# Spreading a delta-rule head's log decays by broadcast transfers instead of TensorE products

## The chip, the cores and the metric

The kernel runs on one core of a Trainium2 chip. The metric is the device time of one execution in microseconds (us). The engines are named as in the profile: PE is TensorE, PEld its weight loads, DVE is VectorE, ACT is ScalarE, POOL is GpSimd and SP is SyncE, which here only issues transfers.

## The reference, cut to what matters

A trunk of two layers on x of 512 tokens by 1024 channels: layer 0 mixes tokens with a bidirectional gated delta rule (GDN), layer 1 with gated linear attention (GLA), and each is followed by an MLP; all of it in float32. The change is in the GDN layer. Per head (8 heads, keys and values of 128) and per direction, in chunks of the sequence:

```python
gc = jnp.cumsum(g.reshape(bn, h, n, CHUNK), axis=-1)          # log decays, summed in the chunk
causal = jnp.tril(jnp.ones((CHUNK, CHUNK), bool))
decay_mat = jnp.exp(jnp.where(causal, gc[..., :, None] - gc[..., None, :], -jnp.inf))
a_mat = jnp.where(strict, jnp.einsum('bhncd,bhnsd->bhncs', kb, k) * decay_mat, 0.0)
lhs = a_mat + jnp.eye(CHUNK, dtype=F32)
sol = lax.linalg.triangular_solve(lhs, rhs, left_side=True, lower=True, unit_diagonal=True)
...
qk = jnp.einsum('bhncd,bhnsd->bhncs', q, k) * decay_mat
q_dec = q * jnp.exp(gc)[..., None]
```

What the change concerns is `decay_mat` and `exp(gc)`: for both, the 512 summed log decays of a direction, which lie one to a token, must be had along the free axis on all 128 partitions, that is spread.

## The kernel before, in words

The tokens are treated as 4 blocks of 128 (NT = 4), both directions side by side, so that one head has U = 8 blocks of 128x128. Projections keep float32 accuracy by three products on TensorE: weights and x are split in a high part (`wh`, `xth`, written by ACT) and a low part (`wl`, `xtl`, by DVE).

`gdn` (L1337) walks the heads in a software pipeline. In iteration i it traces `recur` of head i-2, `solve` of head i-1, `project` of head i and `finish` of head i-2. A scheduler then orders the instructions of every engine's queue from the traced program by what each needs and by priority; an engine's queue is executed strictly in that order. `issue_after` puts an instruction behind another one in this order.

`project` (L1423) makes the four projections of a head (k, q, v, z) and their short convolutions (`conv`, ACT and DVE); after k and q comes `rows` (L1463). There PE transposes k and q blocks (`ktp`), ACT takes sums of squares (`junk`) and the logarithm `lnr`, and DVE makes `rw`, the log decay row of each token and direction (L1488). DVE splits `rw` into three bf16 parts (`rsp`, L1490 to L1496), PE transposes these in four blocks (`rtp`, L1499), and ACT copies the result to `rt`, 6 partitions by 512 (L1501).

`solve` (L1519) begins with the k by k products (`kk`) and, per direction, a product of a constant selector `sel` with `rt` (`ep`, L1534), which spreads the row over 128 partitions in PSUM. ACT takes its exponential as `qd` (L1536) and DVE multiplies it by q. A second product per direction (L1549) adds to the same `ep` the constant triangle `mi` of zeros and very negative numbers; ACT takes `E`, the decay matrix, as eight exponentials from it (L1553), each with a bias per token (`cj`). DVE multiplies E by `kk` (`at`, L1555), ACT rounds it to fp16 (`ath`, L1557).

Then the inverse: 4x4 blocks by three small rounds (`hp`, L1569, with `dc`), their transposes (`xp`, L1585; `Xd`, L1587), and five levels of doubling, 4 to 64. At each level PE makes three sets of eight products `lv` (L1614): one set from `ath` and `Dd`, which ACT or DVE copies to `pz` (L1628 up to 32, L1644 at 64), and two with `pz`, from which `Dd` and `Xd` are updated; at the last level by two ACT copies into `Dd` (L1649) and two of DVE into `Xd` (L1651). Each set waits for the one before. Then comes a correction step (`nw`, L1660 and L1661), the q by k products, and `qke`, E times these.

`recur` (L1687) runs the chunk recurrence with `m` products (L1708), on ACT `vd` (L1723), `vn` (L1726) and `sn` (L1734), and ends with the output products `op`, which use `qke` and `qd`. `finish` (L1749) normalises them (`fo`, L1762) and transposes (`otp`).

SP's queue carries the weights, 512 KB a transfer. In this stage POOL works only at the start, on constant masks (L1170).

Of the kernel before, what the change touches and what calls it, by code (L numbers as in the profile page):

```python
# [17 lines left out]
P = 128  # L18
S = 512
D = 1024  # L20
KT = D // P
NT = S // P
# [1096 lines left out]
NEG = -1e30  # L1119


class GdnConst:


    def __init__(self, c, pool, w_in, w_g, a_log, dt_bias, conv_w, norm_g, x):
        self.c, self.pool = c, pool
# [43 lines left out]
    def masks(self):  # L1170
        c, pool = self.c, self.pool
        G = c.nc.gpsimd
        self.idb = pool.tile([P, P], BF16, name="idb", bufs=1)
        G.tensor_copy(self.idb, c.ident)
        self.idh = pool.tile([P, P], F16, name="idh", bufs=1)
        G.tensor_copy(self.idh, c.ident)

        sf = pool.tile([6, 2, P], F32, name="self", tag="E", bufs=2)
        G.memset(sf, 0.0)
        for s in range(3):  # L1180
            G.affine_select(out=sf, in_=sf, compare_op=ALU.not_equal, fill=1.0, base=-2 * s,
                            pattern=[[-1, 2], [0, P]], channel_multiplier=1)
        self.sel = pool.tile([6, 2, P], BF16, name="sel", bufs=1)
        G.tensor_copy(self.sel, sf)
        self.mi = [pool.tile([P, P], BF16, name=f"mi{d}", bufs=1) for d in range(2)]
        for d in range(2):
            t = pool.tile([P, P], F32, name="tri", tag="cf", bufs=2)
            self.tri(t, d, False, 0.0, NEG)
            G.tensor_copy(self.mi[d], t)

        self.nd = pool.tile([P, P], F32, name="nd", bufs=1)
        G.tensor_scalar(self.nd, c.ident, -1.0, 1.0, ALU.mult, ALU.add)
# [144 lines left out]
def gdn(c, w_in, conv_w, a_log, dt_bias, norm_g, w_out, ln_g, ln_b, x, xt, w_next):  # L1337
    tc, nc = c.tc, c.nc
    w_in, w_g = w_in
    with c.banks(ch=2, pj=3, tp=1, ac=2), tc.tile_pool(name="gdn", bufs=1) as pool:  # L1340
        g = GdnConst(c, pool, w_in, w_g, a_log, dt_bias, conv_w, norm_g, xt)
# [9 lines left out]
        def load_z(hf):  # L1351
            if hf:
                tl = pool.tile([P, NT, S], F32, name="z", tag="sil", bufs=3)
            else:
                tl = heads[-1].next.kq
                more = [heads[-1].t2(tag, n).rearrange("p n i -> p (n i)") for tag, n in (("kt", 3), ("qd", 4))]
# [30 lines left out]
class GdnHead:  # L1387
# [30 lines left out]
    def new_tile(self):  # L1418
        self.sil = self.pool.tile([P, 4, S], F32, name="sil", tag="sil", bufs=3)
        self.kq = self.sil[:, 2:4, :]  # L1420
        return self.sil[:, 0:2, :]

    def project(self, done):  # L1423

        c, pool, g, h = self.c, self.pool, self.g, self.h
# [4 lines left out]
        for i, ci in enumerate((A_H + h, h, 2 * A_H + h, 3 * A_H + h)):  # L1430
            if h == 0 and i == 0:
                ps = g.k0
            else:
                with g.then() if h == 0 else contextlib.nullcontext():
                    wh, wl = c.wcols(self.w_in, ci * P)
                ps = c.bank([P, S], F32, name="pj" + "kqvz"[i], tag="pj")
                for k in range(KT):
                    c.mm3(ps, wh[:, k, :], wl[:, k, :], c.xth[:, k, :], c.xtl[:, k, :], k == 0, k == KT - 1)
                    if h == 0 and (i, k) == (3, 6):
                        g.sums()  # L1440
                        yield from rows
# [12 lines left out]
            yield 0.69, 0.0  # L1454
            if i == 1:
                rows = self.rows(done)
                if h:
                    yield from rows
                else:
                    next(rows)  # L1460
                    next(rows)

    def rows(self, done):  # L1463
# [18 lines left out]

        rw = c.small.tile([P, NT, 2], F32, name="rw", tag="rw")
        self.cj = cj = c.small.tile([P, NT, 2], F32, name="cj", tag="cj")
        lnk = lnr[:, 0, :].unsqueeze(2).to_broadcast([P, NT, 2])
        V.scalar_tensor_tensor(rw, lnk, -0.5, g.gc[:, :, :, h], ALU.mult, ALU.add)  # L1488

        rs = c.small.tile([P, NT, 6], BF16, name="rsp", tag="rsp")  # L1490
        r1 = c.small.tile([P, NT, 2], F32, name="r1", tag="r1")
        V.tensor_copy(rs[:, :, 0:2], rw)
        V.tensor_tensor(r1, rw, rs[:, :, 0:2], ALU.subtract)
        V.tensor_copy(rs[:, :, 2:4], r1)
        V.tensor_tensor(r1, r1, rs[:, :, 2:4], ALU.subtract)
        V.tensor_copy(rs[:, :, 4:6], r1)  # L1496
        rtp = self.bank("rtp", BF16, tag="tp")
        for n in range(NT):
            T.transpose(rtp[:6, n, :], rs[:, n, :], g.idb)  # L1499
# [19 lines left out]
    def solve(self, done):  # L1519
# [8 lines left out]
            T.matmul(kk[:, n, :], self.kc(n), self.kc(n), start=True, stop=True)  # L1528
        yield 0.9, 0.3

        eps, self.qd = [], []
        for d in range(2):
            ps = self.bank("ep")
            T.matmul(ps, g.sel[:, d, :], self.rt, start=True, stop=True)  # L1534
            x = self.t2("qd", 4)
            A.activation(x, ps, AF.Exp)  # L1536
            V.tensor_tensor(x, self.kq[:, 1, :].rearrange("p (n i) -> p n i", n=NT), x, ALU.mult)
            self.qd.append(x)
            eps.append(ps)
        yield 0.63, 1.4  # L1540

        ath, atl = t8("ath", 1), t8("atl", 1)
        kks = self.t2("on", 2)
        V.tensor_tensor(kks, kk, g.nd.unsqueeze(1).to_broadcast([P, NT, P]), ALU.mult)
        a4 = t8("a4", 1)
        ex, ats = [], []
        with c.in_order(mybir.EngineType.PE):
            for d in (1, 0):
                T.matmul(eps[d], g.idb, g.mi[d].unsqueeze(1).to_broadcast([P, NT, P]), start=False, stop=True, skip_group_check=True)  # L1549
        for d, ps in enumerate(eps):  # L1550
            e = self.t2("E", 2)
            for n in range(NT):
                A.activation(e[:, n, :], ps[:, n, :], AF.Exp, bias=self.cj[:, n, d:d + 1])  # L1553
# [92 lines left out]
        ps = prod(xd, pd, 64, 0)  # L1646
        px = prod(pd, xd, 64, 1)
        for d in range(2):
            A.copy(dd[row(1 - d), dirs[d], row(d)], ps[row(1 - d), d, :, :])  # L1649
# [37 lines left out]
    def recur(self, done):  # L1687
# [51 lines left out]
        self.op = op = self.bank("op", tag="ch")  # L1739
        for n in (1, 2, 0, 3):  # L1740
            mm = [(self.qke[d][:, n, :], vns[d][n]) for d in range(2)]
            mm += [(self.qd[d][:, n, :], states[d][n]) for d in range(2) if states[d][n] is not None]
# [103 lines left out]
```

## Time and profile before

| | us |
|---|---|
| three runs | 1327.30, 1327.93, 1328.49 |
| median | 1327.93 |
| profiled execution, its own time | 1328.52 |
| its span in the profile | 1326.6 |
| delta-rule stage with its preparation, in the span | from the start to about 410 |

The trace is of one execution; the span runs from its first instruction to its last, and the 1.9 us between it and the execution's own time lie around it. "Busy" counts an engine's instructions, and PE's matmuls are pipelined, so that each is recorded longer than the step to the next one; a product's cost on PE is therefore read from start to start. In a group's row the numbers behind the bar are busy time, mean ns of one instruction, and idle time before with its releaser.

### The profile page before, as it was taken

The page shows a single profiled execution, that of the slowest core. Times are in us where ns is not written, and L with a number is a line of the kernel's source. Part 1 is how long each engine was busy: PE and PEld are TensorE (multiplying, and loading weights), DVE is VectorE, ACT ScalarE, POOL GpSimd, SP SyncE. Part 2 cuts the span into 40 slices and gives each one's busy share as a digit, 9 for nine tenths or more (in the row PEclk, how much of TensorE's full clock was granted, in tenths as well). Part 3 has the DMA queues.
Part 4 walks back from the last instruction along what each step waited for, and adds up shares of the span by engine and source line. Part 5 has one row for each costly group of instructions (what it writes and reads, how often), then busy time and mean ns, then how long its engine had stood idle before and what let it go on. Part 6 is the DMA issues. An engine that isn't in the chain of part 4 may idle for free.

```text
span 1326.6 us, 22309 instructions
## 1 busy us (share of the span) xinstructions
PE 1307.4 (99%) x8659; PEld 1113.2 (84%) x8659; DVE 1107.7 (83%) x1823; ACT 805.2 (61%) x1598; POOL 124.8 (9%) x177
## 2 busy tenths in 40 slices
PE   9999999999999999999999999999999999999996
PEld 7777877787777889999998888888889889999985
DVE  7787888888668988989988787967879789989887
ACT  4757666767643666566667754654456466666656
POOL 5000000000000910101102200000001001101021
PEclk9999999999999999999999999999999999999998
DMA  5210120211222585675648521111216465657465
GB/s 181 96 49 33 49 65 33 64 49 57 73 99 85 189 178 154 156 191 153 151 150 170 149 90 64 65 63 64 95 64 213 105 193 154 149 172 161 142 143 143
DMA packets 44045, 154.36 MB, mean 116 GB/s; under 512 B 5419, under 2 KB 5795, under 8 KB 43939
## 3 DMA queue, kind: packets, MB, share of 16 engines
q1 hardware_dynamic: 32163, 110.85, 24.9%
q0 software_dynamic: 11776, 42.08, 16.1%
q8 instruction: 68, 1.11, 0.3%
q14 instruction: 38, 0.31, 0.1%
HBM read 113.99 MB, written 2.10 MB: 88 GB/s over the span
## 4 chain that ended last, share of the span: by engine, by line
PE 92%; ACT 3%; DVE 3%; issue 1%; DVEq 0%; POOL 0%; ACTq 0%; POOLq 0%
PE fx L128 3%; PE fx L130 3%; PE fx L129 3%; PE pX L130 3%; PE pX L129 3%; PE pX L128 3%; PE pjv L128 3%; PE pjv L129 3%; PE pjv L130 3%; PE m L1708 3%; PE fyz L128 3%; PE fyz L129 3%; PE fyz L130 3%; PE pY L129 2%; PE pY L128 2%; PE pY L130 2%
## 5 line engine op out<-in xcount | busy, mean ns | idle before, releaser
L102 ACT CAST wh<-wst 128x1024 fp32r<-128x1024 f32 x152 | 159.4, 1049 | 110.3 <-PE fyz L129 35.3
L107 DVE TENSOR_TENSOR wl<-wst,wh 128x1024 fp32r<-128x1024 f32 x150 | 184.3, 1229 | 42.2 <-ACT wh L102 41.9
L107 DVE TENSOR_TENSOR w2l<-w2r,w2h 128x1024 fp32r<-128x1024 f32 x92 | 112.3, 1221 | 24.0 <-ACT w2h L102 23.8
L102 ACT CAST w2h<-w2r 128x1024 fp32r<-128x1024 f32 x94 | 98.5, 1048 | 47.4 <-PE pX L130 16.2
L415 POOL DMA_DIRECT2D w2r<-w2r x56 | 48.5, 892 | 493.9 <-DVE w2l L107 247.3
L102 ACT CAST ah<-h 128x1024 fp32r<-128x1024 f32 x56 | 58.9, 1052 | 40.8 <-PE pX L129 18.1
L464 DVE TENSOR_TENSOR wst<-wst 128x512 f32<-128x512 f32 x120 | 79.8, 685 | 0.4
L107 DVE TENSOR_TENSOR al<-h,ah 128x1024 fp32r<-128x1024 f32 x56 | 68.3, 1220 | 5.1 <-ACT ah L102 4.8
L130 PE MATMUL pX<-w2h,al 128*128 128x512 f32 x168 | 66.2, 394 | 0.0
L129 PE MATMUL pX<-w2l,ah 128*128 128x512 f32 x168 | 66.1, 393 | 0.0
L128 PE MATMUL pX<-w2h,ah 128*128 128x512 f32 x168 | 65.8, 392 | 0.0
L128 PE MATMUL pjv<-wh,xth 128*128 128x512 f32 x128 | 54.7, 427 | 0.0
L128 PE MATMUL fx<-xth,wh 128*128 128x256 f32 x192 | 53.6, 279 | 0.0
L130 PE MATMUL fx<-xh,wl 128*128 128x256 f32 x192 | 53.6, 279 | 0.0
L130 PE MATMUL fyz<-xh,wl 128*128 128x256 f32 x192 | 53.6, 279 | 0.0
L128 PE MATMUL fyz<-xh,wh 128*128 128x256 f32 x192 | 53.6, 279 | 0.0
L128 PE MATMUL fx<-xh,wh 128*128 128x256 f32 x192 | 53.5, 278 | 0.0
L129 PE MATMUL fx<-xl,wh 128*128 128x256 f32 x192 | 53.5, 278 | 0.0
L130 PE MATMUL fx<-xth,wl 128*128 128x256 f32 x192 | 53.4, 278 | 0.0
L129 PE MATMUL fx<-xtl,wh 128*128 128x256 f32 x192 | 53.4, 278 | 0.0
L129 PE MATMUL fyz<-xl,wh 128*128 128x256 f32 x192 | 53.4, 278 | 0.0
L129 PE MATMUL pj<-xtl,wh 128*128 128x256 f32 (+1 forms) x160 | 52.0, 326 | 0.2 <-DVE xtl L194 0.2
(538 smaller groups left out, 4320.7 us busy)
## 6 DMA issues: line engine op xcount, KB each, us to landing
wst<-in_w SPq DMA_DIRECT2D x68, 512.0 KB, 4.3
w2r<-in_w SPq DMA_DIRECT2D x60, 512.0 KB, 4.0
w2r<-w2r POOLq DMA_DIRECT2D x56, 512.0 KB, 5.3
wst<-in_a_in SPq DMA_DIRECT2D x32, 512.0 KB, 3.3
wst<-in_b_vr SPq DMA_DIRECT2D x16, 512.0 KB, 3.3
wst<-in_a_out SPq DMA_DIRECT2D x8, 512.0 KB, 3.3
wst<-in_b_in SPq DMA_DIRECT2D x8, 512.0 KB, 3.3
wst<-in_b_out SPq DMA_DIRECT2D x8, 512.0 KB, 3.3
```

The source lines that it names most:

```text
L102: h = nc.scalar.copy(hi, src)
L107: self.halves = h, nc.vector.tensor_tensor(lo, src, hi.bitcast(F32), ALU.subtract)
L128: mm(ps, ah, bh, start=start, stop=False, **kw)
L129: mm(ps, ah, bl, start=False, stop=False, **kw)
L130: self.last_mm = mm(ps, al, bh, start=False, stop=stop, **kw)
L415: nc.gpsimd.dma_start(blocks[a + (q,)], blocks[b + (q,)], accum_op=ALU.add)
L464: plus = lambda a, b: V.tensor_tensor(a, a, b, ALU.add)
L1708: T.matmul(ps[:, d, :], *ops(d), start=True, stop=True)
```

## The change

The bf16 split, the selector products and the mask products go, with their constants (`idb`, `sel`, `mi`). The two triangles of 0 and very negative numbers are made once in float32 (`later`) and written four times side by side to DRAM (`laterd`) by POOL's queue at the start. Per head:

- SP's queue loads `E` (two directions by 512 per partition, float32) from `laterd`, after the q projection.
- PE makes one float32 transpose of `rw` (`rtp`, 8 partitions by 128), ACT copies it to `rt`, and ACT's queue writes `rt` to DRAM (`row`, 4 KB).
- POOL's queue adds `row`, broadcast to all 128 partitions, to `E` (an accumulating transfer), and then writes the same broadcast into `qd`.
- The eight exponentials of `E` work in place in SBUF. For all heads but the first they are put behind `solved`, the last `Dd` copy of the previous head.
- The exponentials of `qd` and the multiplication by q are traced later, behind the copy of `Xd`.
- The convolutions of k and q, the Silu, and `rows` get a higher priority in the scheduler (`soon`) for all heads but the first.

Buffers: `E` keeps two slots for two heads (both directions in one tile), `qd` likewise; before, `E` had two slots of one direction.

```diff
@@ masks
-        self.idb = pool.tile([P, P], BF16, name="idb", bufs=1)
-        G.tensor_copy(self.idb, c.ident)
...
-        self.mi = [pool.tile([P, P], BF16, name=f"mi{d}", bufs=1) for d in range(2)]
+        later = pool.tile([P, 2, P], F32, name="later", bufs=1)
         for d in range(2):
-            t = pool.tile([P, P], F32, name="tri", tag="cf", bufs=2)
-            self.tri(t, d, False, 0.0, NEG)
-            G.tensor_copy(self.mi[d], t)
+            self.tri(later[:, d, :], d, False, 0.0, NEG)
+        self.later = self.dram.tile([P, 2, NT, P], F32, name="laterd", bufs=1)
+        for n in range(NT):
+            G.dma_start(self.later[:, :, n, :], later)
@@ GdnHead
+    def soon(self, n=350):
+        return self.c.tc.high_priority(offset=n) if self.h else contextlib.nullcontext()
@@ project
             if i < 3:
-                self.conv(kq[:, i, :] if i < 2 else self.v, ps, ci)
+                with self.soon(250) if i < 2 else contextlib.nullcontext():
+                    self.conv(kq[:, i, :] if i < 2 else self.v, ps, ci)
...
-                c.exp_ln_after(A.activation(t, t, AF.Silu))
+                with self.soon():
+                    c.exp_ln_after(A.activation(t, t, AF.Silu))
             yield 0.69, 0.0
             if i == 1:
+                self.e = pool.tile([P, 2, NT, P], F32, name="E", tag="E", bufs=2)
+                c.nc.sync.dma_start(self.e, g.later)
                 rows = self.rows(done)
                 if h:
-                    yield from rows
+                    with self.soon():
+                        yield from rows
@@ rows
-        V.tensor_copy(rs[:, :, 0:2], rw)
-        V.tensor_tensor(r1, rw, rs[:, :, 0:2], ALU.subtract)
-        V.tensor_copy(rs[:, :, 2:4], r1)
-        V.tensor_tensor(r1, r1, rs[:, :, 2:4], ALU.subtract)
-        V.tensor_copy(rs[:, :, 4:6], r1)
-        rtp = self.bank("rtp", BF16, tag="tp")
-        for n in range(NT):
-            T.transpose(rtp[:6, n, :], rs[:, n, :], g.idb)
-        self.rt = pool.tile([6, S], BF16, name="rt", tag="rt", bufs=2)
-        A.copy(self.rt, rtp[:6, :, :].rearrange("p n i -> p (n i)"))
+        rtp = self.bank("rtp", shape=(2 * NT, P), tag="tp")
+        T.transpose(rtp, rdn.rearrange("p d n -> p (d n)"), c.ident)
+        rt = pool.tile([2 * NT, P], F32, name="rt", tag="rt", bufs=2)
+        A.copy(rt, rtp)
+        row = g.dram.tile([2 * NT, P], F32, name="row", tag="row", bufs=3)
+        self.qd = pool.tile([P, 2, NT, P], F32, name="qd", tag="qd", bufs=2)
+        c.nc.scalar.dma_start(row, rt)
+        every = row.rearrange("u p -> (u p)").partition_broadcast(P)
+        c.nc.gpsimd.dma_start(self.e.rearrange("p d n i -> p (d n i)"), every, accum_op=ALU.add)
+        c.nc.gpsimd.dma_start(self.qd.rearrange("p d n i -> p (d n i)"), every)
@@ solve
-        for d in range(2):
-            ps = self.bank("ep")
-            T.matmul(ps, g.sel[:, d, :], self.rt, start=True, stop=True)
-            x = self.t2("qd", 4)
-            A.activation(x, ps, AF.Exp)
-            V.tensor_tensor(x, self.kq[:, 1, :].rearrange("p (n i) -> p n i", n=NT), x, ALU.mult)
...
-        with c.in_order(mybir.EngineType.PE):
-            for d in (1, 0):
-                T.matmul(eps[d], g.idb, g.mi[d].unsqueeze(1).to_broadcast([P, NT, P]), start=False, stop=True, skip_group_check=True)
-        for d, ps in enumerate(eps):
-            e = self.t2("E", 2)
-            for n in range(NT):
-                A.activation(e[:, n, :], ps[:, n, :], AF.Exp, bias=self.cj[:, n, d:d + 1])
+        for d in range(2):
+            e = self.e[:, d, :, :]
+            with c.tc.issue_after(self.solved.ins) if h else contextlib.nullcontext():
+                for n in range(NT):
+                    A.activation(e[:, n, :], e[:, n, :], AF.Exp, bias=self.cj[:, n, d:d + 1])
...
         A.copy(xd, xp)
+        for d in range(2):
+            x = self.qd[:, d, :, :]
+            A.activation(x, x, AF.Exp)
+            V.tensor_tensor(x, self.kq[:, 1, :].rearrange("p (n i) -> p n i", n=NT), x, ALU.mult)
...
-            A.copy(dd[row(1 - d), dirs[d], row(d)], ps[row(1 - d), d, :, :])
+            self.next.solved = A.copy(dd[row(1 - d), dirs[d], row(d)], ps[row(1 - d), d, :, :])
```

How the queues move is read from the order of each engine's instructions in the built program; line numbers behind the change are its own. The first place is PE's queue in one head of the pipeline before, at the products that spread and mask (`m_...` are the recurrence's, `pjq` the next head's q projection):

```order
L1534 MATMUL ep<-rt,sel 128x512
L128 MATMUL pjq<-xth,wh 128x512
L129 MATMUL pjq<-xtl,wh 128x512
...
L1534 MATMUL ep<-rt,sel 128x512
...
L1549 MATMUL ep<-mi_304,idb 128x512
L1708 MATMUL m_2275<-vd,kt 128x128
...
L1549 MATMUL ep<-mi_303,idb 128x512
```

With the change none of these four stands in PE's queue. In their place is one transpose per head, which stands among the levels of the previous head. From it to that head's first `nw` PE has, in head 3, 23 projection products of 512 columns, 9 products of 128 columns and 64 level products; heads 4, 5 and 6 have the same numbers. In head 0 it has 48 projection products and 4 `kk` between the transpose and the first `hp`. The beginning and the end of head 3's piece:

```order
L130 MATMUL pjz<-xth,wl 128x512
L128 MATMUL pjz<-xth,wh 128x512
L1494 MATMUL rtp<-ident,rw 8x128
L129 MATMUL pjz<-xtl,wh 128x512
...
L1758 MATMUL otp<-ident,fo 128x128
L129 MATMUL pjk<-xtl,wh 128x512
L130 MATMUL pjk<-xth,wl 128x512
...
L1652 MATMUL nw<-Dd,ath 128x128
```

So the row is made before the previous head's inverse is finished, where before it was made at about that inverse's end. The third place is ACT's queue in a head of the middle. Before, from the last level of the head in `solve` on:

```order
L1644 ACTIVATE pz_141<-lv 64x4x64
L1649 CAST Dd<-lv 64x4x64 x2
L1501 COPY rt<-rtp 6x512
L1696 COPY vt<-ktp 128x512
L102 CAST wh<-wst 128x1024
L1762 ACTIVATE fo<-op,ors 128x128 x4
L1536 ACTIVATE qd<-ep 128x512 x2
L1723 ACTIVATE vd<-m_2264,kds 128x128
```

and with the change (`pz_143` is the last level's buffer, `pz_141` the one before it):

```order
L1496 COPY rt<-rtp 8x128
L1499 DMA row<-rt 8x128
L102 CAST wh<-wst 128x1024
L1620 CAST pz_141<-lv 32x4x32 x4
...
L1688 COPY vt<-ktp 128x512
...
L1636 ACTIVATE pz_143<-lv 64x4x64
L1578 ACTIVATE qd<-qd 128x512
L1754 ACTIVATE fo<-op,ors 128x128
L1641 CAST Dd<-lv 64x4x64 x2
L1754 ACTIVATE fo<-op,ors 128x128 x3
L1541 ACTIVATE E<-E,cj 128x128 x8
```

The copy of `rt` moves from behind the `Dd` copies to ahead of the last two levels; one exponential of `qd`, which needs POOL's second transfer of the new head, now stands ahead of the previous head's `Dd` copies, and the eight of `E` stand in one block behind them. Heads 3 to 6 have this order. In head 2 the first `qd` exponential stands ahead of `pz_141`; in head 1 both stand behind `E`; in head 7 the first stands ahead of `Dd` again, behind a Silu with its two table loads, and PE has 30 products of 512 columns between its transpose and `nw`. On POOL the two transfers of each head follow one another, with nothing between them.

More of the change, by code (lines that the diff above doesn't have):

```diff
@@ L1122, with __init__ @@
 class GdnConst:
-    def __init__(self, c, pool, w_in, w_g, a_log, dt_bias, conv_w, norm_g, x):
-        self.c, self.pool = c, pool
+    def __init__(self, c, pool, dram, w_in, w_g, a_log, dt_bias, conv_w, norm_g, x):
+        self.c, self.pool, self.dram = c, pool, dram
         nc = c.nc
@@ L1172, in masks @@
         G = c.nc.gpsimd
-        self.idb = pool.tile([P, P], BF16, name="idb", bufs=1)
-        G.tensor_copy(self.idb, c.ident)
         self.idh = pool.tile([P, P], F16, name="idh", bufs=1)
         G.tensor_copy(self.idh, c.ident)
[L1178 to L1184, printed above, removed]
-        self.mi = [pool.tile([P, P], BF16, name=f"mi{d}", bufs=1) for d in range(2)]
+        later = pool.tile([P, 2, P], F32, name="later", bufs=1)
         for d in range(2):
-            t = pool.tile([P, P], F32, name="tri", tag="cf", bufs=2)
-            self.tri(t, d, False, 0.0, NEG)
-            G.tensor_copy(self.mi[d], t)
+            self.tri(later[:, d, :], d, False, 0.0, NEG)
+        self.later = self.dram.tile([P, 2, NT, P], F32, name="laterd", bufs=1)
+        for n in range(NT):
+            G.dma_start(self.later[:, :, n, :], later)
         self.nd = pool.tile([P, P], F32, name="nd", bufs=1)
@@ L1339, in gdn @@
     w_in, w_g = w_in
-    with c.banks(ch=2, pj=3, tp=1, ac=2), tc.tile_pool(name="gdn", bufs=1) as pool:
-        g = GdnConst(c, pool, w_in, w_g, a_log, dt_bias, conv_w, norm_g, xt)
+    with c.banks(ch=2, pj=3, tp=1, ac=2), tc.tile_pool(name="gdn", bufs=1) as pool, \
+            tc.tile_pool(name="gdr", bufs=1, space=bass.MemoryType.DRAM) as dram:
+        g = GdnConst(c, pool, dram, w_in, w_g, a_log, dt_bias, conv_w, norm_g, xt)
         hi = [c.big.tile([P, 2, S], F32R, name=f"oh{t}", tag=f"xt{t}") for t in range(NT)]
@@ L1355, in load_z @@
                 tl = heads[-1].next.kq
-                more = [heads[-1].t2(tag, n).rearrange("p n i -> p (n i)") for tag, n in (("kt", 3), ("qd", 4))]
+                more = [heads[-1].t2("kt", 3).rearrange("p n i -> p (n i)"),
+                        pool.tile([P, 2, S], F32, name="qd", tag="qd", bufs=2)[:, 0, :]]
             for t in range(NT):
@@ L1481, in rows @@
         A.activation(lnr, ssp, AF.Ln, bias=c.bias[RMS_EPS])
-        rw = c.small.tile([P, NT, 2], F32, name="rw", tag="rw")
+        rdn = c.small.tile([P, 2, NT], F32, name="rw", tag="rw")
+        rw = rdn.rearrange("p d n -> p n d")
         self.cj = cj = c.small.tile([P, NT, 2], F32, name="cj", tag="cj")
@@ L1488, in rows @@
         V.scalar_tensor_tensor(rw, lnk, -0.5, g.gc[:, :, :, h], ALU.mult, ALU.add)
-        rs = c.small.tile([P, NT, 6], BF16, name="rsp", tag="rsp")
-        r1 = c.small.tile([P, NT, 2], F32, name="r1", tag="r1")
-        V.tensor_copy(rs[:, :, 0:2], rw)
-        V.tensor_tensor(r1, rw, rs[:, :, 0:2], ALU.subtract)
-        V.tensor_copy(rs[:, :, 2:4], r1)
-        V.tensor_tensor(r1, r1, rs[:, :, 2:4], ALU.subtract)
-        V.tensor_copy(rs[:, :, 4:6], r1)
-        rtp = self.bank("rtp", BF16, tag="tp")
-        for n in range(NT):
-            T.transpose(rtp[:6, n, :], rs[:, n, :], g.idb)
-        self.rt = pool.tile([6, S], BF16, name="rt", tag="rt", bufs=2)
-        A.copy(self.rt, rtp[:6, :, :].rearrange("p n i -> p (n i)"))
+        rtp = self.bank("rtp", shape=(2 * NT, P), tag="tp")
[8 more added lines that the diff above has]
+        c.nc.gpsimd.dma_start(self.qd.rearrange("p d n i -> p (d n i)"), every)
         V.scalar_tensor_tensor(cj, lnk, -0.5, g.lg[:, :, :, h], ALU.mult, ALU.add)
@@ L1741, in recur @@
             mm = [(self.qke[d][:, n, :], vns[d][n]) for d in range(2)]
-            mm += [(self.qd[d][:, n, :], states[d][n]) for d in range(2) if states[d][n] is not None]
+            mm += [(self.qd[:, d, n, :], states[d][n]) for d in range(2) if states[d][n] is not None]
             for i, (l, r) in enumerate(mm):
```

4 lines of the change are left out of this document (removed).

## The prediction

> **What bounds the kernel now.** I read the page's busy shares and chain first, to see which engine sets the end.
>
> ```profile
> span 1326.6 us, 22309 instructions
> PE 1307.4 (99%) x8659; PEld 1113.2 (84%) x8659; DVE 1107.7 (83%) x1823; ACT 805.2 (61%) x1598; POOL 124.8 (9%) x177
> PE 92%; ACT 3%; DVE 3%; issue 1%; DVEq 0%; POOL 0%; ACTq 0%; POOLq 0%
> ```
>
> PE is busy 99% of the span and is 92% of the chain that ended last. The change touches only the delta-rule stage, so its share is read from windows inside that stage (columns: time, then PE, weight load, DVE, ACT and POOL busy, granted clock, DMA share, GB/s) and from PE's waits over the whole of it, 18 to 420 us.
>
> ```profile
> 220.00:260.00 40.00, 39.66 (x367) 32.22 (x366) 32.97 (x74) 27.50 (x81) 0.00 (x0) 1.00 0.13 41
> 260.00:300.00 40.00, 39.86 (x360) 31.75 (x359) 33.25 (x73) 25.83 (x76) 0.00 (x0) 1.00 0.16 54
> ...
> PE lv L1614 <- ACT pz L1628: 1.7, 6, 0.4
> PE nw L1660 <- ACT Dd L1649: 0.8, 2, 0.6
> ```
>
> About one head passes per 40 us. PE lacks work for 0.1 to 0.3 us of it, at the full granted clock; the two largest of the named waits make 2.5 us in 400, both on ACT. POOL does nothing there and the transfer engines are at 0.13 to 0.16. So PE time that is taken away should come out of the end, and any wait put into ACT's queue ahead of a level of the inverse comes into it.
>
> **The products that go.** PE's timeline of one head (start, duration; I take start to start, since products overlap):
>
> ```profile
> 210.78 0.39 PE L129 MATMUL pjq<-xtl,wh 128*128 128x512 f32 x1
> 211.10 0.39 PE L1499 MATMUL rtp<-idb,rsp 128*6 128x128 bf16 x4
> 211.42 0.50 PE L130 MATMUL pjq<-xth,wl 128*128 128x512 f32 x1
> 211.76 0.39 PE L128 MATMUL pjq<-xth,wh 128*128 128x512 f32 x1
> 211.98 0.40 PE L129 MATMUL pjq<-xtl,wh 128*128 128x512 f32 x1
> ...
> 212.46 0.60 PE L1694 MATMUL ktp<-ident,sil 128*128 128x128 f32 x4
> 212.99 0.60 PE L1534 MATMUL ep<-rt,sel 6*128 6x512 bf16 x2
> 213.52 0.50 PE L128 MATMUL pjq<-xth,wh 128*128 128x512 f32 x1
> 213.85 0.40 PE L129 MATMUL pjq<-xtl,wh 128*128 128x512 f32 x1
> ...
> 214.98 0.59 PE L1549 MATMUL ep<-mi,idb 128*128 128x512 bf16 x2
> 215.22 0.58 PE L130 MATMUL pjq<-xth,wl 128*128 128x512 f32 x1
> 215.64 0.40 PE L128 MATMUL pjq<-xth,wh 128*128 128x512 f32 x1
> ```
>
> The four transposes hold 211.10 to 211.42, 0.32 us; the two spreading products 212.99 to 213.52, 0.53; the two mask products 214.98 to 215.22, 0.24. Together 1.09 us. A plain projection product takes 0.22 (211.76 to 211.98; elsewhere 0.23); beside the removed ones they take 0.32, 0.34, 0.33 and 0.42 (from 210.78, 211.42, 213.52 and 215.22), which is 0.53 more. If all of that goes too, it is 1.62. I take 1.4 a head, 11.2 us for eight. One new f32 transpose per head costs a quarter of the four at 212.46 (0.53 to the next start), 0.13, so 1.0 for eight. **The gain is 10.2 us, from 7.7 to 12.** The five small DVE instructions a head that go with the split are worth nothing by themselves: DVE has 7 us of 40 idle and PE, not DVE, is short; were that cover gone, five at about the 0.21 us of ACT's small `neg` below would be 1 us a head.
>
> **The transfers that come.** They replace something that took one PE product and no transfer, and the trace of before has none like them. Per head ACT's queue writes 4 KB to DRAM (`row`), then POOL issues an accumulating broadcast of 512 KB into E and one of 512 KB into qd. Nearest rows (issues in POOL's timeline, landings in the transfer view of 689 to 697 us, KB and us; then the page):
>
> ```profile
> 691.31 0.57 POOL L614 DMA_DIRECT2D ln<-in_ln_b  x1 [40.02 <-PE fyz L130]
> ...
> ln<-in_ln_b POOLq DMA_DIRECT2D x1, 512.0 KB, 4.2
> ln<-in_ln_g POOLq DMA_DIRECT2D x1, 512.0 KB, 5.0
> gst<-in_b_gates SPq DMA_DIRECT2D x1, 128.0 KB, 2.1
> ...
> w2r<-w2r POOLq DMA_DIRECT2D x2, 512.0 KB, 7.1
> ...
> L415 POOL DMA_DIRECT2D w2r<-w2r x56 | 48.5, 892 | 493.9 <-DVE w2l L107 247.3
> w2r<-w2r POOLq DMA_DIRECT2D x56, 512.0 KB, 5.3
> out<-xt SPq DMA_DIRECT2D x4, 256.0 KB, 3.5
> ```
>
> Call X the time from the issue of `row` to the landing of qd. The small transfer takes 2.1 (`gst`, a read) to 3.5 (`out`, a write of 64 times the bytes); I take 2.4, since 4 KB is nearer to the first. POOL's issue of the accumulating one takes 0.57 to 0.89; I take 0.9. The second of a pair from POOL landed after 5.0; 4.2 is the first, 5.3 the accumulating kind. So X is 2.4 + 0.9 + 5.0 = 8.3 us, at least 2.1 + 0.57 + 4.2 = 6.9, at most 3.5 + 0.9 + 5.3 = 9.7.
>
> The page "DMA: Bandwidth & Descriptors" of the Trainium skill, section "Anatomy of one DMA — SWDGE (gpsimd) path", fits a POOL transfer as about 2.0 us plus the bytes over 436 GB/s; that is an estimated 3.2 us for 512 KB, against 4.2 to 5.3 in the rows above, and by it X would be about 6.1 and everything hidden. The same section says that the receipt is slowest where the target is DRAM, which speaks against the trip of `row`; no run here shows such a small write yet.
>
> **What waits for them.** In ACT's new order for heads 3 to 6, `qd<-qd` and one `fo` stand ahead of the last level's two `Dd` copies, and PE's `nw` of the head before needs `Dd`. ACT's prices (us busy, mean ns) and PE's stretch there:
>
> ```profile
> L1762 ACT ACTIVATE fo<-op,ors 128x128 f32<-128x128 f32 x32 | 9.3, 372 | 2.9 <-DVE ors L211 2.8
> L1536 ACT ACTIVATE qd<-ep 128x512 f32<-128x512 f32 x16 | 9.3, 612 | 8.2 <-PE ep L1534 8.2
> L1553 ACT ACTIVATE E<-ep,cj 128x128 f32<-128x128 f32 x64 | 18.9, 404 | 3.8 <-PE ep L1549 3.8
> L1649 ACT CAST Dd<-lv 64x256 f16<-64x256 f32 x16 | 5.9, 367 | 2.7 <-PE lv L1614 2.3
> L1505 ACT ACTIVATE neg<-rw 128x8 f32<-128x8 f32 x8 | 1.7, 209 | 3.7 <-DVE rw L1488 3.6
> ...
> 197.51 0.39 PE L129 MATMUL pjz<-xtl,wh 128*128 128x512 f32 x1
> 198.20 0.39 PE L1614 MATMUL lv<-pz,Xd 128*128 128x64 f16 x8 [0.30 <-ACT pz L1628]
> 198.43 0.40 PE L1614 MATMUL lv<-Xd,pz 128*128 128x64 f16 x8
> ...
> 200.46 0.40 PE L130 MATMUL pjz<-xth,wl 128*128 128x512 f32 x1
> 201.23 0.66 PE L1473 MATMUL ktp<-ident,sil 128*128 128x128 f32 x4 [0.37 <-ACT junk L1478]
> ...
> 202.74 0.40 PE L130 MATMUL pjk<-xth,wl 128*128 128x512 f32 x1
> 203.21 0.22 PE L1660 MATMUL nw<-Dd,ath 128*128 128x128 f16 x1
> ```
>
> From the new transpose, `nw` can start after 0.6 (0.39 for the product, 0.21 for a copy as small as `neg`), X, and 0.61 + 0.37 + 2 x 0.37 = 1.7: at 10.6 us. Meanwhile PE has by the new order 23 projection products, 9 of 128 columns and 64 level products in 8 sets, in each of heads 3 to 6: 23 x 0.23 + 9 x 0.13 + 8 x 0.23 = 8.3 us. Before has in such a stretch gaps of 0.46 (197.51 to 198.20, less 0.23), 0.54 (200.46 to 201.23) and 0.24 (202.74 to 203.21), and some 0.3 more in lengthened steps, so it takes about 9.8 anyway. What X adds is X + 2.3 - 9.8, **0.8 us a head** at 8.3 and nothing below 7.5. Head 2 has its first qd exponential ahead of a level still earlier in the queue, and I count it the same: 5 x 0.8 = 4.0.
>
> Head 0 has no earlier head: from its transpose to the first block product `hp` PE has 48 projection and 4 `kk` products, 11.5 us; E lands about when qd does less half a microsecond (0.6 + 7.8), eight exponentials follow (8 x 0.404 = 3.2) and three steps of 128x512 on DVE and ACT, some 1.7 at about `qd<-ep`'s 0.6: 13.3, so 1.8 us late. At the start four POOL writes of masks compete with the loads of x, for which ACT waits:
>
> ```profile
> 8.81 1.05 ACT L1242 CAST xth<-xt 128x1024 fp32r<-128x1024 f32 x1 [1.49 <-DMA xt<-in_xt]
> ```
>
> I take 0.5 of that, from 0 to 1.5. Heads 1 and 7 are free: head 1's exponentials stand behind `Dd`, and head 7 has 30 projection and output products as cover instead of 23, worth 1.6 us. The SP queue's eight loads of E stand between weight loads; the idle transfer engines take them, and E's slot was read a head earlier. The 64 exponentials of E only change place: they were among `vd` and `sn`, now they are one block of 3.2 us behind `Dd`, and ACT has 12 of 40 us idle. **The loss is 4.0 + 1.8 + 0.5 = 6.3 us**, 0.9 at the least X and 14.7 at the most.
>
> **The sum.** 1328.5 (the profiled execution, 0.6 above the median of the runs) - 10.2 + 6.3 = 1324.6, which is **1324 us** against the median. Each microsecond of X is worth 6 us, five heads and head 0; loss and gain are equal at X of 8.9.
>
> **The rivals.** *A, the forecast*: gain mostly kept, X between 7.7 and 8.9, 1320 to 1328; 0.42. *B, slower*: the pair lands late because E's load, the weights and both broadcasts share the transfer engines; `w2r` took 7.1 where it met other loads. X is then 9.4 (from there on it is slower by more than can be told) to 3.5 + 0.9 + 7.1 = 11.5; at 10.3 it costs 5 x 2.8 + 3.8 + 1 = 18.8, and the time is about 1336. For it: ACT's queue is strict and PE has no other product ready. Against: the transfer engines are 0.16 busy. 0.27. *C, given back*: the chain of levels through DVE and ACT sets the head's period, and what PE no longer does turns into waits before `lv` and `nw`; 1328. For it: those waits are there already. Against: 0.1 us idle in 40. 0.15. *D, all hidden*: X at or below 7.5, as from the least row; loss 0.9, about 1318.5. 0.16.
>
> **How the numbers follow.** Under 0.2%, 2.7 us, a measurement of this kernel can't tell from no change. Two thirds of A and all of D are faster: 0.28 + 0.16 and a little of C, 0.46. C, the upper part of A and the lower edge of B are the same, 0.26; the rest of B is slower, 0.28. The range leaves out the far end of B and of D: 1314 to 1337; A's own is 1320 to 1328.
>
> **What would show it.** Right: `ep` gone from PE, no lengthened steps, and in each of heads 2 to 6 one PE wait of about a microsecond before `nw` or `lv`, ended by ACT, whose `qd` waited for a POOL transfer; X near 8.3. D shows no such wait, B one of 2 us or more. C shows `lv` waits longer with qd landed in time. The gain is wrong if the projection products beside the gaps don't return to 0.23.

## The result, and the profile after

The change makes the kernel slower: 1345.95 us (four runs, 1343.63 to 1351.16) against 1327.96 us before, a ratio of 1.0141 with a 95% interval of 1.0111 to 1.0172. The profiled execution took 1343.63 us. From the page of the profile after, the span, the busy row, the shares of the chain that ended last, and four rows of the transfers:

```profile
span 1341.9 us, 22215 instructions
PE 1303.2 (97%) x8603; PEld 1114.9 (83%) x8603; DVE 1102.6 (82%) x1783; ACT 805.5 (60%) x1598; POOL 137.1 (10%) x189
PE 83%; DMA 6%; DVE 6%; ACT 4%; issue 1%; POOL 0%; DVEq 0%; POOLq 0%; SPq 0%; ACTq 0%
...
wst<-in_a_in SPq DMA_DIRECT2D x32, 512.0 KB, 4.4
E<-laterd SPq DMA_DIRECT2D x8, 512.0 KB, 3.4
E<-row POOLq DMA_DIRECT2D x8, 512.0 KB, 5.2
qd<-row POOLq DMA_DIRECT2D x8, 512.0 KB, 7.0
```

PE has less to do, yet the span is longer: transfers now make 6% of the chain, where none stood before, and PE's share fell from 92% to 83%. PE's waits over the delta-rule stage, 8 to 430 us, say where (what waited, for what; total, times, longest):

```profile
PE otp L1758 <- ACT fo L1754: 9.3, 5, 3.5
PE lv L1606 <- ACT pz L1620: 5.2, 4, 4.4
PE hp L1557 <- DVE a L1546: 5.0, 1, 5.0
```

Before, the largest of these sums was 1.7. The long waits in all three rows go back to ACT waiting for one of POOL's transfers: `hp` (head 0) to E's, `lv` (head 2) and `otp` to qd's. ACT's rows in heads 0 and 2 (start, duration; in brackets the idle time before and what ended it):

```profile
56.14 2.15 ACT L1541 ACTIVATE E<-E,cj 128x128 f32<-128x128 f32 x7 [8.89 <-DMA E<-row]
...
123.53 0.63 ACT L1578 ACTIVATE qd<-qd 128x512 f32<-128x512 f32 x1 [5.62 <-DMA qd<-row]
124.18 1.06 ACT L1620 CAST pz<-lv 32x128 f16<-32x128 f32 x4
```

In head 3 of the change, ACT's timeline:

```profile
170.54 0.38 ACT L1636 ACTIVATE pz<-lv 64x256 f16<-64x256 f32 x1 [1.86 <-PE lv L1606]
173.65 0.63 ACT L1578 ACTIVATE qd<-qd 128x512 f32<-128x512 f32 x1 [2.73 <-DMA qd<-row]
174.30 0.37 ACT L1754 ACTIVATE fo<-op,ors 128x128 f32<-128x128 f32 x1
174.69 0.76 ACT L1641 CAST Dd<-lv 64x256 f16<-64x256 f32 x2
```

and PE's at the same place:

```profile
171.84 0.40 PE L1606 MATMUL lv<-Xd,pz 128*128 128x64 f16 x8
174.72 0.36 PE L1758 MATMUL otp<-ident,fo 128*128 128x128 f32 x1 [2.48 <-ACT fo L1754]
174.81 0.70 PE L129 MATMUL pjk<-xtl,wh 128*128 128x512 f32 x1
175.31 0.63 PE L130 MATMUL pjk<-xth,wl 128*128 128x512 f32 x1
```

ACT stands 2.73 us before `qd<-qd` because POOL's second transfer has not landed. `fo` and the `Dd` copies are ready behind it and cannot pass. PE has finished the last level and is idle for 2.48 us, and when it goes on, a projection product takes 0.50 us to the next start instead of 0.23. That second loss is the clock: windows before, in, and after another such stall (head 4), and behind a stall of 1.56 us (head 6); the granted clock is the third number from the right:

```profile
218.00:223.00 5.00, 1.48 (x21) 0.86 (x19) 0.58 (x3) 1.01 (x3) 0.00 (x0) 0.97 0.83 288
223.00:227.00 4.00, 3.98 (x29) 3.40 (x30) 2.37 (x6) 3.83 (x13) 0.00 (x0) 0.61 0.01 2
227.00:231.00 4.00, 4.00 (x28) 3.30 (x27) 3.95 (x8) 2.68 (x5) 0.00 (x0) 1.00 0.24 80
...
312.00:316.00 4.00, 3.42 (x35) 2.83 (x35) 3.44 (x7) 3.93 (x15) 0.00 (x0) 1.00 0.22 91
```

After the long stall PE is busy for 4 us at 0.61 of its clock; after the short one it is at 1.00 at once. By head, from the trace of the change (us; X is from the issue of `row` to the landing of qd, clock lost is one minus the granted clock, summed over the 9 us after the stall in steps of 1 us):

| head | `row` to E's issue | E lands after | qd lands after | X | PE idle | clock lost |
|---|---|---|---|---|---|---|
| 0 | 3.4 | 7.8 | 8.4 | 12.4 | 5.0 | 2.0 |
| 1 | 2.3 | 5.2 | 6.3 | 9.2 | none | 0 |
| 2 | 3.6 | 5.7 | 7.0 | 11.2 | 4.4 | 2.6 |
| 3 | 1.7 | 5.0 | 8.1 | 10.4 | 2.5 | 1.7 |
| 4 | 2.3 | 4.9 | 8.2 | 11.1 | 3.5 | 1.5 |
| 5 | 1.8 | 5.3 | 7.0 | 9.4 | 1.5 | 0 |
| 6 | 1.7 | 5.2 | 6.8 | 9.1 | 1.6 | 0 |
| 7 | 1.9 | 5.3 | 7.0 | 9.5 | 0.5 | 0 |

The landing of `row` itself is not recorded, so its column runs to POOL's issue. In heads 1 to 7 the profile names a DVE instruction, not `row`, as what ended POOL's wait, so what else is in that column stays open.

Heads 2 to 6 were idle for 13.4 us, head 0 for 5.0, and 7.9 us more went with the clock: 26.3 us. The profiled execution before, less the 10.2 us of the forecast gain, plus 26.3, is 1344.6; measured were 1343.63.

### The profile page after: what moved, and what is told of

Read it like the earlier page. It is cut to its first block, busy times and chain, and to the rows that moved or that the text cites. A ratio compares the mean times of both kernels' runs of the same rounds, so it can differ in the third digit from the quotient of the medians.

```text
span 1341.9 us, 22215 instructions
## 1 busy us (share of the span) xinstructions
PE 1303.2 (97%) x8603; PEld 1114.9 (83%) x8603; DVE 1102.6 (82%) x1783; ACT 805.5 (60%) x1598; POOL 137.1 (10%) x189
## 4 chain that ended last, share of the span: by engine, by line
PE 83%; DMA 6%; DVE 6%; ACT 4%; issue 1%; POOL 0%; DVEq 0%; POOLq 0%; SPq 0%; ACTq 0%
PE fx L128 3%; PE fx L130 3%; PE pX L130 3%; PE pX L129 3%; PE fx L129 3%; PE pX L128 3%; PE m L1700 3%; PE pjv L130 3%; PE pjv L128 3%; PE pjv L129 3%; DMA qd<-row 3%; PE fyz L130 3%; PE fyz L128 3%; PE fyz L129 2%; PE pY L129 2%; PE pY L130 2%
```

## The experiments

The first theory after the result was this: the gain is there, and what the kernel lost is PE idle behind ACT's queue, in which qd's exponential waits for its transfer, plus a lower clock after the long stalls. The rivals were that the levels' chain gives the gain back, that the weight loads and not the pair itself make qd late, and that the raised priority is the culprit.

**qd behind Dd.**

```diff
-            A.activation(x, x, AF.Exp)
+            with c.tc.issue_after(self.solved.ins) if h else contextlib.nullcontext():
+                A.activation(x, x, AF.Exp)
```

> The change with one edit: the two exponentials of qd are also put behind the previous head's last Dd copy, so that nothing on ACT waits for POOL's second transfer ahead of Dd. Theory (late qd holds ACT's queue, and a PE idle of 2.5 us or more is followed by some 5 us at a lower granted clock): the idle time of 13.4 us in heads 2 to 6 and about 5.8 us of low clock behind it go, head 0 stays as it is (5.0 us idle and about 2 us of low clock), so 1343.6 - 19.2 = about 1324 us, with the granted clock at 1.00 from 100 us on. Rival 1 (the place in ACT's queue is not what matters; E is late as well, and the exponentials of E behind Dd hold vd and vn instead): 1335 or more, with PE waits of over 2 us before m products. Rival 2 (the levels' own chain eats what PE no longer does): about 1330 to 1335, with longer waits before lv.

Measured: 1324.95 us, ratio 0.9978 (0.9969 to 0.9988). The sum was right to a microsecond. X stayed between 8.3 and 11.5 us in heads 1 to 7, so the transfers were no earlier; only what stands behind them in ACT's queue changed. PE's waits of the stage:

```profile
PE hp L1557 <- DVE a L1546: 4.7, 1, 4.7
PE ktp L1475 <- ACT sil L1452: 0.9, 3, 0.6
PE m L1701 <- DVE sn L1729: 0.5, 1, 0.5
```

Only head 0's stall is left. Both rivals fall: no wait before `m` is longer than 0.5 us, and those before `lv` sum to 0.5.

**qd first.**

```diff
-        c.nc.gpsimd.dma_start(self.e.rearrange("p d n i -> p (d n i)"), every, accum_op=ALU.add)
+        to_e = lambda: c.nc.gpsimd.dma_start(self.e.rearrange("p d n i -> p (d n i)"), every, accum_op=ALU.add)
+        if not h:
+            to_e()
         c.nc.gpsimd.dma_start(self.qd.rearrange("p d n i -> p (d n i)"), every)
+        if h:
+            to_e()
```

> The change with one edit: for heads 1 to 7 POOL issues the broadcast into qd first and the accumulating one into E second. The scheduler then puts both qd exponentials ahead of Dd. If the landing time of qd is what PE waits for: qd lands about 2 + 5.2 = 7.3 us after the row's issue instead of 9.1 to 11.2, the idle time per head falls from 1.5 to 4.4 to at most 1 us, no low clock follows in heads 2 to 6, and the time is 1325 to 1331 us. Rival (weight loads and both broadcasts share the transfer engines, whichever is issued first lands no earlier than now): 1340 or more.

Measured: 1335.36 us, ratio 1.0062 (1.0043 to 1.0081), a miss between the two. The landing did what was expected, from the page's transfer rows:

```profile
E<-row POOLq DMA_DIRECT2D x8, 512.0 KB, 7.8
qd<-row POOLq DMA_DIRECT2D x8, 512.0 KB, 4.7
```

The two have changed places: whichever is second lands two to three microseconds later. X of qd was 6.1 to 7.1 us in six of heads 1 to 7 and 9.1 in one. But then E is the late one, and the scheduler had put six of its exponentials ahead of `fo`. ACT's timeline in head 3 of this run:

```profile
170.08 0.76 ACT L1645 CAST Dd<-lv 64x256 f16<-64x256 f32 x2 [0.53 <-PE lv L1610]
173.90 1.86 ACT L1545 ACTIVATE E<-E,cj 128x128 f32<-128x128 f32 x6 [3.07 <-DMA E<-row]
175.67 1.11 ACT L1758 ACTIVATE fo<-op,ors 128x128 f32<-128x128 f32 x4
```

PE idled 2.34 us for `fo`. Making one transfer earlier moved the wait to the other.

**One broadcast only.** E is left with a constant triangle, without its decays; only the landing is read.

```diff
-            self.tri(later[:, d, :], d, False, 0.0, NEG)
+            self.tri(later[:, d, :], d, False, -1000.0, NEG)
...
-        c.nc.gpsimd.dma_start(self.e.rearrange("p d n i -> p (d n i)"), every, accum_op=ALU.add)
```

> What makes qd land 6.3 to 8.2 us after its issue: the change without the accumulating broadcast into E (E keeps only the constant triangle, the decays are left out of it), so that qd's broadcast is the only one of a head; the order on ACT may shift, only the landing is read. If the pair's first transfer holds up the second, qd lands after 4.5 to 5 us, as the first of the pair did. If the weight loads that are issued a microsecond or two later do it, it still takes 6.5 us or more.

From this kernel's page, and then from the transfer view of its window 239 to 248 us, in which two weight loads fall as well:

```profile
qd<-row POOLq DMA_DIRECT2D x8, 512.0 KB, 4.2
```

```profile
wst<-in_a_in SPq DMA_DIRECT2D x2, 512.0 KB, 3.2
qd<-row POOLq DMA_DIRECT2D x1, 512.0 KB, 4.0
```

Alone, qd lands 4.2 us after its issue (median), and one after 4.0 with a weight load issued 2.1 us behind it. All eight landed after 3.9 to 4.9 us, though in seven heads a weight load was issued between 0.7 us before qd's transfer and 2.7 us behind it; here the weight loads by themselves did not make qd late. The pair makes it late without them: in head 1 of the change, with no weight load issued from 8.4 us before to 5.6 us behind it, the second landed after 6.3 us. But the rival is not gone. In heads 2 to 6, with a weight load issued 1.1 to 1.7 us behind, the second took 6.8 to 8.2 us, and in the second run of the next experiment a lone transfer into qd (head 7), with three other loads issued between 1.1 us before and 0.4 us behind it, took 7.2. No edit separated the two shares. The one run took 1321.96 us.

**The gain alone.** Two runs took E's and qd's transfers from a constant row, traced at the head's first projection, so that nothing should wait for them; the heads' own decays are left out of E and qd. In the first, qd's exponentials were free to run early.

```diff
-        c.nc.scalar.dma_start(row, rt)
-        every = row.rearrange("u p -> (u p)").partition_broadcast(P)
...
+        every = g.row0.rearrange("u p -> (u p)").partition_broadcast(P)
...
+        r0 = pool.tile([2 * NT, P], F32, name="r0", tag="rt", bufs=2)
+        G.memset(r0, -1000.0)
+        self.row0 = self.dram.tile([2 * NT, P], F32, name="row0", bufs=1)
+        G.dma_start(self.row0, r0)
```

> The gain by itself. The transfers into E and qd stay (same number and size), but they take a constant row from DRAM that is written at the start, and are issued at the head's first projection, so nothing on PE's path waits for them; the row of the head is transposed and copied, but not written to DRAM and not used (the head's own decays are left out of E and qd). Theory (10.2 us of PE time saved, all losses come from the late transfers): about 1328.5 - 10 = 1318 us, from 1316 to 1321, clock 1.00. Rival (given back: the levels' chain sets the period): 1325 to 1328 us, with longer lv waits.

Measured: 1326.85 us, 0.9991 (0.9982 to 1.0001), where 1318 was expected. Taken by its time alone this would have been the rival's. The trace shows another cause: at the start four exponentials of qd stood ahead of the gates' copy `yr` and waited for transfers that share the start with other loads.

```profile
20.77 2.22 ACT L1580 ACTIVATE qd<-qd 128x512 f32<-128x512 f32 x4 [2.92 <-DMA qd<-row]
22.90 1.03 ACT L102 CAST wh<-wst 128x1024 fp32r<-128x1024 f32 x1
23.83 0.57 ACT L1274 COPY yr<-bap 64x512 f32<-64x512 f32 x1
```

PE lost 4.67 us there and 3.6 of clock: the experiment had made a stall of its own. It was repeated with the exponentials behind `Dd`.

> The constant-row run again, without the stall it had of its own at the start: there the exponentials of qd, made free to run early, waited on ACT for the start's transfers ahead of the gates (4.67 us idle and 3.6 us of low clock). Now the exponentials of qd stay behind Dd (head 0: behind the copy of rt) and E and qd are loaded a projection later for the first head. The head's own decays are left out of E and qd as before. Theory (about 10 us of PE time saved, losses only from late transfers): 1326.85 - 8.3 = about 1318.5 us, from 1316 to 1321. Rival (given back to the levels' chain): 1325 or more with nothing idle at the start.

Measured: 1321.74 us, 0.9953 (0.9938 to 0.9968), 3 us above the expectation, outside its range, and below the rival's bound. It still has two waits of 1.5 us at the start, for weights, and a clock of 0.83 behind them (the waits, then a window):

```profile
PE pjq L128 <- ACT wh L102: 1.5, 1, 1.5
PE pjq L130 <- DVE wl L107: 1.5, 1, 1.5
```

```profile
24.00:30.00 6.00, 6.00 (x24) 4.74 (x23) 5.72 (x12) 0.79 (x2) 4.50 (x12) 0.83 0.82 269
```

These are 3.0 and 1.7 us. Without them it would be at 1317, and no `lv` or `nw` wait was longer than 0.3 us, so nothing shows that the levels' chain gave anything back. This correction is an estimate; the next run needs none.

**Head 0 by products.** Head 0's row is spread by eight small products again, with the triangle added by DVE; in the first run with qd behind `Dd`, in the second in the change as it is.

```diff
+        self.tri2 = later
...
-                c.nc.sync.dma_start(self.e, g.later)
+                if h:
+                    c.nc.sync.dma_start(self.e, g.later)
...
+        for d in range(0 if h else 2):
+            ps = self.bank("ep")
+            for n in range(NT):
+                u = d * NT + n
+                T.matmul(ps[:, n, :], c.ident[:2 * NT, u:u + 1].to_broadcast([2 * NT, P]), self.rt, start=True, stop=True)
+            V.tensor_tensor(self.e[:, d, :, :], ps, g.tri2[:, d, :].unsqueeze(1).to_broadcast([P, NT, P]), ALU.add)
+            A.activation(self.qd[:, d, :, :], ps, AF.Exp)
...
```

> The first experiment (qd behind Dd) with one more edit: head 0 alone is spread by products again (eight of 128 columns from its transposed row, the triangle added by DVE, E's and qd's transfers of head 0 left out), so that its exponentials do not wait for a transfer. In the first experiment head 0 had 4.67 us of PE idle time and 3.1 us of clock lost behind it. Theory: 1324.95 - 7.8 + 0.9 for the products = about 1318 us, clock 1.00 throughout. Rival (head 0's first block product waits for its exponentials whichever way the row comes, or the next late step takes its place): 1322 or more.

Measured: 1317.80 us, 0.9922 (0.9908 to 0.9937), as expected, and the fastest of all: 0.8% below the kernel before. PE's largest waits of its stage, and from the page its share of the chain:

```profile
PE lv L1621 <- ACT pz L1635: 1.4, 5, 0.4
PE nw L1667 <- ACT Dd L1656: 0.5, 1, 0.5
```

```profile
PE 90%; DVE 4%; ACT 4%; DMA 1%; issue 1%; SPq 0%; DVEq 0%; ACTq 0%
```

> The change itself with head 0 alone spread by products, everything else as in the change, qd's exponential ahead of Dd too. Theory (losses of head 0 and of heads 2 to 6 add up): head 0's 5.0 us idle and 2.0 us of clock go, 0.9 comes for the products: 1345.95 - 6.1 = about 1340 us, with the stalls of heads 2 to 6 as they were. Rival (one stall follows from the other, the pipeline is late from head 0 on): 1335 or less.

Measured: 1337.00 us, 1.0081 (1.0060 to 1.0103), 3 us below the expectation and 2 above the rival's bound. The four waits of `otp` for `fo` were 11.3 us against 9.3, one of them 5.0 in a head where qd landed 8.6 us after its issue; heads 2 and 4 in turn lost less. Head 0's stall was gone. The expected 1340 lies within the spread of this kernel's runs (1336.5 to 1342.1), so the parts add up as far as this can tell.

**The priorities and E's place.** The change without the raised priorities (`soon` returns nothing), and the mended kernel without them:

```diff
     def soon(self, n=350):
-        return self.c.tc.high_priority(offset=n) if self.h else contextlib.nullcontext()
+        return contextlib.nullcontext()
```

> The change without the raised priorities (soon). The row is then made around or behind the previous head's last level, qd's exponentials stand behind Dd, and the exponentials of E stand among vd and vn. If a late transfer in a strict queue is the cause, the wait only moves: E lands some 8 us after the row, and ACT holds vd and vn for it, so that PE idles before m, op or hp; 1340 to 1355 us, with low clock after the stalls. Rival (the raised priority is what does the harm, by pulling qd ahead of Dd): no wait of over 1 us, 1325 us or less.

> The mended kernel (qd behind Dd, head 0 by products) without the raised priorities. The row is made around the previous head's last level; the exponentials of E then stand on ACT ahead of vd, before their transfer can have landed. In the run of the change without the priorities the waits of m for vd were 10.8 us and the clock lost after two of them 3.4 us. Theory (any strict queue that meets the transfers too early pays; the priority is what buys their time): 1317.8 + about 14 = 1332 us, from 1327 to 1336, with waits of m for vd. Rival (with qd and head 0 mended the priorities are worth nothing): 1320 or less.

Measured: 1340.01 us (1.0085, 1.0068 to 1.0102), at the lower end of what was expected, and 1348.16 us (1.0159, 1.0142 to 1.0176), 12 us beyond the expected range. In both the wait has moved to E, whose exponentials now stand ahead of `vd` and `fo`: ACT in one head of the first, then of the second,

```profile
184.65 1.86 ACT L1541 ACTIVATE E<-E,cj 128x128 f32<-128x128 f32 x6 [3.31 <-DMA E<-row]
186.41 0.60 ACT L1715 ACTIVATE vd<-m,kds 128x128 f32<-128x128 f32 x2
```

```profile
218.15 1.57 ACT L1554 ACTIVATE E<-E,cj 128x128 f32<-128x128 f32 x5 [5.18 <-DMA E<-row]
219.63 1.11 ACT L1769 ACTIVATE fo<-op,ors 128x128 f32<-128x128 f32 x4
```

So the priority is not what loses the time. In the change as it stands it does cost 6 us (1345.95 against 1340.01): without it the idle times over 0.7 us fall from 18.5 to 15.3 us and the clock lost behind them from 7.9 to 5.1. But once qd and head 0 are mended it buys the transfers time: without it the mended kernel loses 30 us, twice what was expected. PE's idle times over 0.7 us in it sum to 18 us, the clock lost behind three of them to 4.7, and a stretch at half clock near the start (21.7 to 25.1 us) costs 1.7; the other 6 us stay open.

Last, E's exponentials free of their place:

```diff
-            with c.tc.issue_after(self.solved.ins) if h else contextlib.nullcontext():
+            with contextlib.nullcontext():
                 for n in range(NT):
```

> The mended kernel without the placement of E's exponentials behind the previous head's last Dd copy: the scheduler puts four to six of them ahead of Dd, in one head ahead of pz of the last level. E lands about 7.6 us after the row's issue (5.0 to 5.5 after its own), so in the working of the prediction nw could start at 0.6 + 7.6 + 4 to 6 times 0.404 + 0.74 = 10.6 to 11.4 us against 9.8: about 1 to 1.6 us a head, more where it stands ahead of pz. Theory: 1317.8 + 6 to 11 = 1324 to 1329 us, with PE waits for Dd and pz on ACT. Rival (E lands in time, only qd is late): 1320 or less.

Measured: 1322.53 us, 0.9960 (0.9945 to 0.9974); 4.7 us above the mended kernel; that is 1.5 us below the expected range and 2.5 above the rival's bound. The waits are short and of the expected kind:

```profile
PE nw L1667 <- ACT Dd L1656: 2.3, 4, 0.7
PE lv L1621 <- ACT pz L1635: 1.9, 4, 1.0
PE otp L1773 <- ACT fo L1769: 1.6, 3, 0.8
```

The placement of E's exponentials is right and worth about 4.7 us; the change has it for E and lacks it for qd.

## Why the prediction was wrong

The forecast, A, said 1324 us; the mechanism of rival B happened, whose price, 1336, was still 10 us short.

**The gain** was right. The mended kernel is 9.8 us below the runs of before, with head 0's products, estimated at 0.9 us, still in it: some 10.7 us without them, against a forecast of 10.2. Rival C falls with it.

**The place of the wait** was right: heads 2 to 6, on ACT, `qd<-qd` ahead of `fo` and `Dd`, PE idle before the products behind them (`otp`, where the forecast named `nw`; in head 2 `lv`). So was the arithmetic around it. X + 2.3 - 9.8 with the measured X of heads 2 to 6 gives 3.7, 2.9, 3.6, 1.9 and 1.6, together 13.6 us; PE was idle for 13.4.

**The step that failed** is the size of X: "The second of a pair from POOL landed after 5.0". In that row no weight load was in flight with the pair, only one 512 KB transfer that POOL issued 1.85 us behind the second, and neither transfer of the pair was an accumulating one. Here the second landed after 6.8 to 8.2 us in heads 2 to 6, on average 7.4. Part of the difference is there without weight loads (6.3 in head 1), where the first of the pair is an accumulating transfer; the rest comes where weight loads are in flight. The other two terms were if anything too high: `row` took 1.7 to 3.6 us to E's issue, 2.2 on average, for 2.4, and POOL's first issue held the second by 0.55, not 0.9. X came to 10.2 on average, outside the stated 6.9 to 9.7 in three of these five heads. The profile page had the warning in a row that the prediction quoted and kept for rival B, `w2r` at 7.1 us where it met other loads; it was the nearest row to a transfer that lands among others, and was priced as the far end.

**Head 0** failed by the same term. With E's measured landing, 11.2 us after the issue of `row`, the prediction's own sum for it (0.6 + 11.2 + 3.2 + 1.7 - 11.5) is 5.2; measured 5.0, forecast 1.8.

**The clock** was left out altogether, the second step that failed. The sums priced an idle PE at its idle time. Four stalls of 2.5 us and more each cost another 1.5 to 2.6 us, 7.9 in all. With X and the clock as measured, and no other number altered, the forecast's sum is 1328.5 - 10.2 + 13.6 + 5.2 + 0.5 + 7.9 = 1345.5 us. Of the 20.9 us that separate this from the forecast's 1324.6, X is 13.0 and the clock 7.9.

**The certainty** was too great on one more count: each microsecond of X was said to be worth 6 us, with balance at 8.9. X was known to no better than 1.4 us either way, so that the sign itself hung on it; by that the chance of B should have been nearer to A's. Two figures of the prediction are slips and change nothing: with its own 2.4 and 0.9, a transfer of 3.2 makes an X of 6.5, not 6.1 (both are below 7.5), and a chance of 0.28 for slower is more than the whole 0.27 of B, of which it is a part.

## What to carry to other kernels

An instruction that waits for a transfer must stand in a strict queue behind everything that is ready earlier; two exponentials moved behind the `Dd` copies turned +1.4% into -0.2%, with the same late transfers. When two transfers are issued in a pair, price the second by what the pair moves together, not by its own size, and look for what is first in the pipeline (head 0 here) and has no earlier work to hide it. Where PE is the bound, the four stalls of 2.5 us and more cost 1.4 to 1.7 times their length, so ask of each possible wait whether it is as long as that.

## What the runs showed of the hardware

**The granted clock after an idle PE.** Over all runs, single idle times of PE up to 1.88 us left the clock at 1.00 (such stalls of 0.7 to 1.9 us stand in nine of the traces; one pair of them is the exception named below); idle times of 2.48 us and more were each followed by 0.5 for about 3 to 7 us, and 1.4 to 3.6 us were lost. Between these it went either way: 2.34 us and 2.41 us were followed by low clock, 2.35 us in another run was not. Two idle times of 1.5 us with 0.7 us of work between them were followed by it too (1.7 us lost). The page "TensorE: Matmul & The Clock Gate" of the Trainium skill, section "Part 1: The HAM clock gate", says that the clock halves after an idle window of about 3.4 us and comes back after about as long a busy one, and that the window runs freely. The half clock and the 3 to 7 us agree with it; the idle time that suffices does not, since 2.3 us did here.

That the window is not tied to the stall can be read from the granted clock. In the change it drops to 0.5 at 58.84, 123.69, 174.89 and 222.68 us, and the distances are 19, 15 and 14 times 3.41 us; each of these stretches lasts 3.41 or 6.83 us. Of the 2.34 us, 1.95 fell into one such window of 3.41 us; the 2.35 us were split by two, 1.10 and 1.25. Between 40 and 1300 us of all twelve traces, each of the 15 windows at full clock in which PE was busy for 1.58 us or less was followed by 0.5; in all others PE was busy for 1.72 us or more, and none of them was. Near the start that does not hold: in three runs a window with PE busy for 1.95 to 2.81 us was followed by 0.5 as well, and why stays open.

**A pair of POOL transfers.** Of two 512 KB transfers issued 0.55 us apart, the first landed after 4.9 to 5.7 us in heads 1 to 7 and the second after 6.3 to 8.2; one alone after 4.2 (median, 3.9 to 4.9). The second is the later one in either order, but the accumulating one takes longer in both places: as the first 4.9 to 5.7 against 4.3 to 5.5 us, as the second 7.1 to 9.5 against 6.3 to 8.2. With no other transfer in flight, in the first run with a constant row, the accumulating one took 4.8 to 5.2 us (four heads) and the plain one 3.8 (one head). The transfer engines were at 0.83 of their time in the stall's window quoted above, where two stretches of 40 us before the change had 0.13 and 0.16: such an average said nothing about the few microseconds that mattered.
